# Four edits at stage borders of a transformer block: transposes, a bank, four small loads and the last scaling

## The chip, the cores and the metric

The kernel runs on one core of one Trainium2 chip. A core has a matrix engine (TensorE, PE in the profile, its weight loads PEld), VectorE (DVE), ScalarE (ACT), GpSimd (POOL) and SyncE (SP), which here only issues loads and stores. Each engine works through its own queue in order. The metric is the device time of one execution in microseconds.

## The reference

One streaming encoder block in float32, on 512 tokens of width 1024 and 16 learned meta tokens ahead of them:

```python
xn = rmsnorm(h, norm_mix_g)
proj = xn @ w_in                        # q, k, v of two attention branches
# branch A: stick-breaking attention, 8 heads of 128
# branch B: differential attention, 8 heads: softmax map 1 - lam * softmax map 2
lam = exp(sum(lam_q1 * lam_k1)) - exp(sum(lam_q2 * lam_k2)) + lam_init
gates = sigmoid(xn @ w_gate + b_gate)
h = h + (gates[0] * (o_sb @ w_br_sb) + gates[1] * (o_df @ w_br_df)) @ w_out
hn = rmsnorm(h, norm_ffn_g)
h = h + (silu(hn @ w_ffn_gate) * (hn @ w_ffn_up)) @ w_ffn_down    # 2816 wide
y = rmsnorm(h, norm_final_g)            # meta tokens dropped
```

## The kernel before, in words

**Products in three parts.** Every float32 operand of a large product is split into a rounded part and the rest (`split`, L77 to L81: ScalarE copies the rounded part, `wh` or `hT_h`, and VectorE subtracts it, `wl` or `hT_l`). `mm3` (L293 to L298) then issues three matmuls for one product: high by high (L296), and the two mixed ones (L297, L298).

**Seven products for eight.** Where a product is cut in 2 by 2 blocks, the kernel forms sums of blocks ahead and needs seven block products instead of eight (`a11`, `a12`, `s1` to `s4`, `a22` by their weight side; `b11`, `b21`, `t1` to `t4`, `b22` by their token side). This is done for k and v of the stick-breaking heads from the third on, for the output projection, for SwiGLU's column tiles 2 to 21 of 22, and for the down projection. Several of the seven add into one PSUM bank, and partial sums are copied out of it between them.

**Stages, in order.** Input norm and transposes; eight stick-breaking heads, then eight differential heads (one loop, `br` and `h`), with the projections of the next head issued between the pieces of the present one; gates and merge; output projection (`out_steps`); norm, and transposes of the normed tokens (`turned`, L1145); SwiGLU's column tiles 0 and 1 as plain products (`early_products`); tiles 2 to 21 with seven products each (`first`, `second`, `third`); down projection (`step`), final norm and stores (`finish`, L1406).

**What sets the order.** The program is written out without loops on the chip. A scheduler orders each engine's queue at build time, by a model of time and by the order in the program; `tc.high_priority(offset=EVAC)` moves an instruction up in that order, and `behind(ins, name)` (L83) adds a dependency on an instruction recorded in `cast`. The scheduler sets the waits as well. PSUM banks are taken in turn from two pools: `mm_tile()` (four of 128x512) and `z_tile()` (two of 128x2x512, so two banks each).

**Weights.** `stream` lists all weight pieces in the order of use. `stage_one` (L186 to L210) issues the load of the next into a staging buffer on SP's queue; `generic` (L222) makes the split of one piece, and its argument `after` can put ScalarE's copy behind another instruction. Position `first_ffn` is the gate piece of column tile 2, so `first_ffn - 1` is the up piece of tile 1; `first_down` is the first piece of the down projection.

**The four places of the change.**

- `turned(tp_)` (L1145 to L1166) transposes the normed tokens `hn` for half `tp_` of them (256 tokens, 8 tiles of 128 features, called k; two transposes a k). For two k at a time it issues four transposes into one bank (L1152) and then, for each k, ScalarE's copy to `hT_h` (L1157) and VectorE's rest to `hT_l` (L1158). After the loop `bf` gets a plain copy (L1163) for the block sums. Two z tiles give four banks; k 0 and 1 share one, 2 and 3 the next, and so on. `turned(0)` is issued as soon as the third token tile is normed, among the last steps of the output projection; `turned(1)` comes after the products of gate and up tile 0 with the first 256 tokens.
- `second` and `third` (L1305 to L1334): in column tile f, the products s2, s3 and a22 add into the bank `e1` of `first`, and s1 and s4 into a z bank `e3`. `qx` and `qy` are copies of e1 after s2 and after s3 (L1310, L1315); `qy` then gets e3 added (L1316). The other column tiles issue a22 ahead of s4; the last one, 21, issues s4 first.
- `df_constants` (L818 to L839) loads the four lambda vectors on SP's queue (L822), into a buffer shared with the heads, and computes lambda from them. The loop calls it at stick-breaking head 4.
- `rstd` (L374) gives 1/sqrt from ScalarE's log and exp and one Newton step on VectorE, as three small instructions: u = r*r*v (L388), u = 1.5 - u/2 (L384), r = r*u (L386). `finish(t)` (L1406) calls it, then scales one half of token tile t on VectorE (L1409) and the other on ScalarE (L1411) and issues a store behind each (L1410, L1412). The last call is that of t = 1.

Of the kernel before, what the change touches and what calls it, by code (L numbers as in the profile page):

```python
# [9 lines left out]
F32 = mybir.dt.float32  # L10
# [6 lines left out]
P = 128  # L17
# [4 lines left out]
KT = D // P  # L22
# [19 lines left out]
def block_kernel(ctx: ExitStack, tc: tile.TileContext, x, meta, norm_mix_g, w_in, w_gate, b_gate,  # L42
# [179 lines left out]
    def generic(n):  # L222
        wh, wl = parts(n)
        split(wh, wl, staged[n], nc.gpsimd if n < 3 else None, after="qy" if n == first_down else None)
        cast["split"] = cast["lo"]
# [148 lines left out]
    def rstd(ss, n=1, scale=1.0 / D, more=None):  # L374
# [5 lines left out]

        def newton(steps=(0, 1, 2)):
            for i in steps:
                if i == 1:
                    nc.vector.tensor_scalar(u, u, -0.5, 1.5, op0=ALU.mult, op1=ALU.add)  # L384
                elif i == 2:
                    nc.vector.tensor_tensor(r, r, u, op=ALU.mult)  # L386
                elif n == 1:
                    nc.vector.scalar_tensor_tensor(u, r, r, v, op0=ALU.mult, op1=ALU.mult)  # L388
                else:
                    nc.vector.tensor_tensor(u, r, r, op=ALU.mult)  # L390
                    nc.vector.tensor_tensor(u, u, v, op=ALU.mult)
            return r

# [422 lines left out]
    var_max = const.tile([P, 1], F32, name="var_max")  # L816

    def df_constants():  # L818
        nc.vector.tensor_scalar(g_sub, pcol[:, 32:33], 1.0 - LAM_INIT, None, op0=ALU.mult)
        lam4 = opool.tile([P, 4, 64], F32, tag="sg1", name="lam4")  # L820
        for i, v in enumerate((lam_q1, lam_k1, lam_q2, lam_k2)):
            nc.sync.dma_start(lam4[:, i], v.broadcast_to([P, 64]))  # L822

        lp = opool.tile([P, 2, 64], F32, tag="sg1", name="lp")
        lv = lam4.rearrange("p (a b) c -> p a b c", b=2)
# [167 lines left out]
    for br in range(2):  # L993
# [151 lines left out]
    def turned(tp_):  # L1145
        cs = slice(tp_ * 256, (tp_ + 1) * 256)
        banks = [z_tile() for _ in range(2)]
        for k in range(0, KT, 2):
            pt = banks[k // 2 % 2][:, k // 4]
            for i in range(2):  # L1150
                for t in range(2):
                    nc.tensor.transpose(pt[:, (2 * i + t) * P:(2 * i + t + 1) * P],  # L1152
                                        hn[:, 2 * tp_ + t, (k + i) * P:(k + i + 1) * P], ident)
            for i in range(2):
                g = g_ffn[:, k + i:k + i + 1]
                p = pt[:, i * 256:(i + 1) * 256]
                nc.scalar.activation(hT_h[:, k + i, cs], p, AF.Copy, scale=g)  # L1157
                nc.vector.scalar_tensor_tensor(hT_l[:, k + i, cs], p, g, hT_h[:, k + i, cs].bitcast(F32),  # L1158
                                               op0=ALU.mult, op1=ALU.subtract)
        for k in range(KT):  # L1160
            p = banks[k // 2 % 2][:, k // 4, k % 2 * 256:(k % 2 + 1) * 256]
            if tp_ == 0:
# [101 lines left out]
    with tc.tile_pool(name="ffn", bufs=1) as fp:  # L1264
# [40 lines left out]
        def second(f):  # L1305
# [6 lines left out]
            product(f, "s1", tsum["t1"], e3, True)  # L1312
            product(f, "s3", tsum["t3"], e1, False)
            with tc.high_priority(offset=EVAC):
                cast["qy"] = nc.scalar.copy(qy, e1)  # L1315
                nc.vector.tensor_tensor(qy, e3, qy, op=ALU.add)  # L1316
            return qx, qy

        def third(f, qx, qy):
            e1, e2, e3, sg = bank[f]  # L1320
            def up():
                product(f, "a22", tsum["t4"], e1, False)
                with tc.high_priority(offset=EVAC):
                    nc.vector.scalar_tensor_tensor(aT[:, f, T1], e1, -1.0, sg[:, T1], op0=ALU.mult, op1=ALU.mult)

            def gate_and_up():
                product(f, "s4", tsum["b22"], e3, False)
                with tc.high_priority(offset=EVAC):
                    nc.vector.tensor_tensor(sg[:, T2], e3, qx, op=ALU.add)
                nc.scalar.activation(sg[:, T2], sg[:, T2], AF.Silu)  # L1330
                nc.vector.scalar_tensor_tensor(aT[:, f, T2], qy, -1.0, sg[:, T2], op0=ALU.mult, op1=ALU.mult)

            for half in (up, gate_and_up) if f < NFF - 1 else (gate_and_up, up):
                half()  # L1334

# [69 lines left out]

        def finish(t):  # L1406
            r = rstd(ssq[t][:, 1:2], more=ssq[t][:, 0:1])()
            o = outs[t]
            nc.vector.tensor_scalar(o[:, 0:512], o[:, 0:512], r, None, op0=ALU.mult)  # L1409
            nc.sync.dma_start(ov[:, t, 0:512], o[:, 0:512])  # L1410
            nc.scalar.activation(o[:, 512:D], o[:, 512:D], AF.Copy, scale=r)  # L1411
            nc.sync.dma_start(ov[:, t, 512:D], o[:, 512:D])  # L1412
# [38 lines left out]
        for ph, (w, b, e) in enumerate(DOWN):  # L1451
# [15 lines left out]
            for t in range(2):  # L1467
                for c0, c1 in ((0, 256), (256, 512)) if ph == 6 and t else ((0, 512),):
# [26 lines left out]
                    elif w == "a22":  # L1495
# [3 lines left out]
                        if c1 == 512:  # L1499
                            finish(t)  # L1500
        inner.close()
# [29 lines left out]
```

## Time and profile before

| what | us |
|---|---|
| median of the runs | 933.06 |
| lowest, highest run | 931.36, 1141.8 |
| the profiled execution's own time | 930.84 |
| its span, first to last instruction | 929.1 |
| TensorE busy | 916.9 |
| VectorE, ScalarE, GpSimd busy | 733.4, 583.6, 168.6 |

In the profile a row of the timeline gives the start in us from the span's start, the duration, the engine, the line, the operation with output and inputs, their shape, and in brackets how long the engine had been idle before and what ended that. Matmuls are pipelined, so their durations overlap and one reads their starts. A row of the stretches gives busy time and number of instructions for each engine, the granted TensorE clock, the share of the DMA engines and GB/s. TensorE is busy for all but 12 us of the span: some at the start, some behind the last matmul, the rest at the borders between stages.

### The profile page before, as it was taken

The numbers are of one execution on the slowest core, as the hardware profiler recorded it, in microseconds if no ns is written. First come the engines' busy times: TensorE is split into PE (matmuls) and PEld (weight loads), VectorE is DVE, ScalarE is ACT, GpSimd is POOL, SyncE is SP. The second block draws the span as 40 slices with busy tenths as digits, with TensorE's granted clock in tenths as the row PEclk, the third lists the DMA queues.
The fourth block names the chain that finished last, engine by engine and source line by source line (L and its number), as shares of the span: only waits on it lengthen the run. The fifth ranks groups of instructions, "written<-read, shape, count | busy, mean of one in ns | idle before, by whom it ended". The sixth has DMA issues, their size and how long they took to land.

```text
span 929.1 us, 16027 instructions
## 1 busy us (share of the span) xinstructions
PE 916.9 (99%) x6009; PEld 835.0 (90%) x6010; DVE 733.4 (79%) x1412; ACT 583.6 (63%) x1102; POOL 168.6 (18%) x199
## 2 busy tenths in 40 slices
PE   8999999999999999999999999999999999999997
PEld 5999999998999899998988888899999999988886
DVE  7988877776677766976663787899888889799975
ACT  7665676676666666666665555775555655576554
POOL 4000121222333343344512000001100000000013
PEclk9999999999999999999999999999999999999999
DMA  8525788778777978799987774427754343276642
GB/s 253 143 72 161 167 185 199 177 167 252 192 191 175 220 168 182 183 208 192 194 207 175 220 262 159 126 79 182 172 129 120 93 135 92 92 271 194 191 148 91
DMA packets 155823, 158.41 MB, mean 171 GB/s; under 512 B 6465, under 2 KB 117218, under 8 KB 155746
## 3 DMA queue, kind: packets, MB, share of 16 engines
q1 hardware_dynamic: 132690, 101.61, 36.1%
q0 software_dynamic: 22896, 55.72, 29.3%
q8 instruction: 47, 0.77, 0.3%
q14 instruction: 30, 0.25, 0.1%
q10 hardware_dynamic: 160, 0.07, 0.0%
HBM read 133.64 MB, written 50.86 MB: 199 GB/s over the span
## 4 chain that ended last, share of the span: by engine, by line
PE 94%; DVE 2%; ACT 2%; issue 1%; DMA 0%; ACTq 0%; DVEq 0%
PE mm L296 22%; PE mm L297 22%; PE mm L298 22%; PE z L296 7%; PE z L298 7%; PE z L297 7%; PE z L563 2%; PE z L696 1%; PE z L695 1%; PE tr L537 1%; DVE wl L81 1%; PE z L584 1%; DMA wst<-in_w_ffn_up_dram 0%; DVE hres L1200 0%; PE mm L855 0%
## 5 line engine op out<-in xcount | busy, mean ns | idle before, releaser
L296 PE MATMUL mm<-xT_h,wh 128*128 128x264 f32 (+2 forms) x656 | 213.6, 326 | 0.5 <-ACT xT_h L898 0.5
L297 PE MATMUL mm<-xT_l,wh 128*128 128x264 f32 (+2 forms) x656 | 213.4, 325 | 0.5
L298 PE MATMUL mm<-xT_h,wl 128*128 128x264 f32 (+2 forms) x656 | 212.6, 324 | 0.0
L78 ACT CAST wh<-wst 128x1024 fp32r<-128x1024 f32 (+1 forms) x147 | 141.4, 966 | 77.4 <-PE mm L297 55.5
L81 DVE TENSOR_TENSOR wl<-wst,wh 128x1024 fp32r<-128x1024 f32 (+1 forms) x147 | 163.3, 1116 | 31.2 <-ACT wh L78 30.9
L297 PEld LDWEIGHTS mm<-xT_l,wh 128*128 128x128 f32 x656 | 123.4, 188 | 10.3 <-DVE xT_l L899 1.3
L298 PEld LDWEIGHTS mm<-xT_h,wl 128*128 128x128 f32 x656 | 123.5, 188 | 10.0
L296 PEld LDWEIGHTS mm<-xT_h,wh 128*128 128x128 f32 x656 | 123.4, 188 | 10.0 <-ACT xT_h L898 0.9
L296 PE MATMUL mm<-hT_h,wh 128*128 128x256 f32 x304 | 83.8, 277 | 0.9 <-ACT hT_h L1157 0.8
L298 PE MATMUL mm<-hT_h,wl 128*128 128x256 f32 x304 | 83.9, 277 | 0.0
L297 PE MATMUL mm<-hT_l,wh 128*128 128x256 f32 x304 | 83.8, 276 | 0.0
L296 PEld LDWEIGHTS mm<-hT_h,wh 128*128 128x128 f32 x304 | 56.9, 188 | 1.3 <-ACT hT_h L1157 1.0
L699 DVE CUSTOM_DVE_ANT_0 pr<-z,bias 128x144 f32<-128x144 f32 (+3 forms) x64 | 30.9, 502 | 34.0 <-PE z L696 31.8
L297 PEld LDWEIGHTS mm<-hT_l,wh 128*128 128x128 f32 x304 | 57.0, 188 | 0.0
L298 PEld LDWEIGHTS mm<-hT_h,wl 128*128 128x128 f32 x304 | 57.0, 188 | 0.0
L296 PE MATMUL mm<-o_h,wh 128*128 128x512 f32 x128 | 52.4, 410 | 0.0
L296 PE MATMUL z<-wh,da 128*128 128x512 f32 (+1 forms) x132 | 50.3, 381 | 0.0
L297 PE MATMUL z<-wl,da 128*128 128x512 f32 (+1 forms) x132 | 50.2, 381 | 0.0
L298 PE MATMUL z<-wh,da 128*128 128x512 f32 (+1 forms) x132 | 50.2, 380 | 0.0
L298 PE MATMUL mm<-o_h,wl 128*128 128x512 f32 x128 | 50.1, 391 | 0.0
L297 PE MATMUL mm<-o_l,wh 128*128 128x512 f32 x128 | 49.9, 390 | 0.0
L151 POOL DMA_DIRECT2D ds<-in_w_ffn_down_dram x36 | 30.2, 841 | 91.7 <-ACT wh L78 62.1
(359 smaller groups left out, 2464.5 us busy)
## 6 DMA issues: line engine op xcount, KB each, us to landing
wst<-in_w_in_dram SPq DMA_DIRECT2D x40, 512.0 KB, 6.3
ds<-in_w_ffn_down_dram POOLq DMA_DIRECT2D x30, 512.0 KB, 6.6
wst<-in_w_ffn_gate_dram SPq DMA_DIRECT2D x22, 512.0 KB, 4.0
wsu<-in_w_ffn_up_dram SPq DMA_DIRECT2D x20, 512.0 KB, 4.0
wst<-in_w_gate_dram SPq DMA_DIRECT2D x16, 512.0 KB, 4.8
y_df<-y_out POOLq DMA_DIRECT2D x32, 256.0 KB, 7.7
slots<-ds SPq DMA_DIRECT2D x13, 512.0 KB, 3.3
os<-in_w_out_dram POOLq DMA_DIRECT2D x12, 512.0 KB, 5.2
```

The source lines that it names most:

```text
L78: cast["last"] = (hi_copy or nc.scalar.copy)(hi, src)
L81: cast["lo"] = (lo_eng or nc.vector).tensor_tensor(lo, src, hi.bitcast(F32), op=ALU.subtract)
L151: tc.add_manual_dep(nc.gpsimd.dma_start(dst, src, **kw).ins, cast["last"].ins.name, paced)
L296: nc.tensor.matmul(ps, lhsT=ah, rhs=bh, start=(start and i == 0), stop=False, skip_group_check=skip)
L297: nc.tensor.matmul(ps, lhsT=ah, rhs=bl, start=False, stop=False, skip_group_check=skip)
L298: nc.tensor.matmul(ps, lhsT=al, rhs=bh, start=False, stop=(stop and i == n - 1), skip_group_check=skip)
L537: nc.tensor.transpose(pt[:, j * P:(j + 1) * P], vT[:, j * P:(j + 1) * P], ident)
L563: nc.tensor.transpose(pt[:, (t - j) * P:(t - j + 1) * P], blocks(t, j * P, (j + 1) * P), ident)
L584: nc.tensor.matmul(ps.rearrange("p (t q) -> p t q", q=P)[:, :, lo_rows:P], lhsT=vf[:, 1], rhs=a_s[:, 0:4 * qn], start=False, stop=True)
L695: nc.tensor.matmul(o, lhsT=q[c][:, qs], rhs=k[c][:, 0, k0:k1], start=True, stop=False)
L696: nc.tensor.matmul(o, lhsT=q[c][:, qs], rhs=k[c][:, 1, k0:k1], start=False, stop=True)
L699: nc.vector.tensor_tensor_reduce(po, zz, bb, scale=1.0, scalar=-3.0e38, op0=ALU.add, op1=ALU.max, accum_out=mx[:, t, c:c + 1])
```

## The change

1. `turned(0)` issues all sixteen transposes first and then the eight pairs of copies; `turned(1)` keeps its order of two k at a time. The last `hT_h` copy of `turned(0)` is recorded, and the weight copy of the last piece ahead of `first_ffn` (the up piece of column tile 1) gets a dependency on it.
2. In the last column tile, a22 gets a bank of its own from `mm_tile()`. The copy of e1 after s3 goes to a buffer `qz`; `qy` is e3 plus `qz` as before, VectorE adds the own bank to `qz`, and that sum takes the place of e1 in the last product with the gate. The order is now a22 ahead of s4 in all column tiles.
3. The four lambda loads move into `df_loads`, called at head 2, with buffers of their own; the computation stays at head 4.
4. In the last `finish` both halves are scaled on VectorE, by r and u as two factors, without the step r = r*u; ScalarE takes no part.

```diff
     def generic(n):
         wh, wl = parts(n)
-        split(wh, wl, staged[n], nc.gpsimd if n < 3 else None, after="qy" if n == first_down else None)
+        split(wh, wl, staged[n], nc.gpsimd if n < 3 else None, after={first_down: "qy", first_ffn - 1: "hT"}.get(n))
...
-        def newton(steps=(0, 1, 2)):
+        def newton(steps=(0, 1, 2), factors=False):
+            steps = steps[0:2] if factors else steps
             for i in steps:
...
-            return r
+            return (r, u) if factors else r
...
+    lams = []
+
+    def df_loads():
+        lams.extend((ap_.tile([P, 4, 64], F32, name="lam4"), ap_.tile([P, 2, 64], F32, name="lp")))
+        for i, v in enumerate((lam_q1, lam_k1, lam_q2, lam_k2)):
+            nc.sync.dma_start(lams[0][:, i], v.broadcast_to([P, 64]))
+
     def df_constants():
+        lam4, lp = lams
         nc.vector.tensor_scalar(g_sub, pcol[:, 32:33], 1.0 - LAM_INIT, None, op0=ALU.mult)
-        lam4 = opool.tile([P, 4, 64], F32, tag="sg1", name="lam4")
-        for i, v in enumerate((lam_q1, lam_k1, lam_q2, lam_k2)):
-            nc.sync.dma_start(lam4[:, i], v.broadcast_to([P, 64]))
-
-        lp = opool.tile([P, 2, 64], F32, tag="sg1", name="lp")
...
+            if (br, h) == (0, 2):
+                df_loads()
             if (br, h) == (0, 4):
                 df_constants()
...
     def turned(tp_):
         cs = slice(tp_ * 256, (tp_ + 1) * 256)
         banks = [z_tile() for _ in range(2)]
-        for k in range(0, KT, 2):
-            pt = banks[k // 2 % 2][:, k // 4]
-            for i in range(2):
+        half = [banks[k // 2 % 2][:, k // 4, k % 2 * 256:(k % 2 + 1) * 256] for k in range(KT)]
+        step = 2 if tp_ else KT
+        for k0 in range(0, KT, step):
+            for k in range(k0, k0 + step):
                 for t in range(2):
-                    nc.tensor.transpose(pt[:, (2 * i + t) * P:(2 * i + t + 1) * P],
-                                        hn[:, 2 * tp_ + t, (k + i) * P:(k + i + 1) * P], ident)
-            for i in range(2):
-                g = g_ffn[:, k + i:k + i + 1]
-                p = pt[:, i * 256:(i + 1) * 256]
-                nc.scalar.activation(hT_h[:, k + i, cs], p, AF.Copy, scale=g)
-                nc.vector.scalar_tensor_tensor(hT_l[:, k + i, cs], p, g, hT_h[:, k + i, cs].bitcast(F32),
+                    nc.tensor.transpose(half[k][:, t * P:(t + 1) * P], hn[:, 2 * tp_ + t, k * P:(k + 1) * P], ident)
+            for k in range(k0, k0 + step):
+                g = g_ffn[:, k:k + 1]
+                hi = nc.scalar.activation(hT_h[:, k, cs], half[k], AF.Copy, scale=g)
+                nc.vector.scalar_tensor_tensor(hT_l[:, k, cs], half[k], g, hT_h[:, k, cs].bitcast(F32),
                                                op0=ALU.mult, op1=ALU.subtract)
+                if tp_ == 0:
+                    cast["hT"] = hi
...
+            qz = quarter("q1") if f == NFF - 1 else qy
             with tc.high_priority(offset=EVAC):
-                cast["qy"] = nc.scalar.copy(qy, e1)
-                nc.vector.tensor_tensor(qy, e3, qy, op=ALU.add)
-            return qx, qy
+                cast["qy"] = nc.scalar.copy(qz, e1)
+                nc.vector.tensor_tensor(qy, e3, qz, op=ALU.add)
+            return qx, qy, qz

-        def third(f, qx, qy):
+        def third(f, qx, qy, qz):
             e1, e2, e3, sg = bank[f]
-            def up():
-                product(f, "a22", tsum["t4"], e1, False)
...
-            def gate_and_up():
-                product(f, "s4", tsum["b22"], e3, False)
...
-            for half in (up, gate_and_up) if f < NFF - 1 else (gate_and_up, up):
-                half()
+            own = mm_tile()[:, 0:256] if f == NFF - 1 else None
+            product(f, "a22", tsum["t4"], e1 if own is None else own, own is not None)
+            with tc.high_priority(offset=EVAC):
+                if own is not None:
+                    nc.vector.tensor_tensor(qz, own, qz, op=ALU.add)
+                nc.vector.scalar_tensor_tensor(aT[:, f, T1], e1 if own is None else qz, -1.0, sg[:, T1],
+                                               op0=ALU.mult, op1=ALU.mult)
+            product(f, "s4", tsum["b22"], e3, False)
...
-        def finish(t):
-            r = rstd(ssq[t][:, 1:2], more=ssq[t][:, 0:1])()
+        def finish(t, last=False):
+            r = rstd(ssq[t][:, 1:2], more=ssq[t][:, 0:1])(factors=last)
             o = outs[t]
+            if last:
+                for cs in (D1, D2):
+                    nc.vector.tensor_scalar(o[:, cs], o[:, cs], *r, op0=ALU.mult, op1=ALU.mult)
+                    nc.sync.dma_start(ov[:, t, cs], o[:, cs])
+                return
...
-                            finish(t)
+                            finish(t, t == 1)
```

More of the change, by code (lines that the diff above doesn't have):

```diff
@@ L1147, in turned @@
         banks = [z_tile() for _ in range(2)]
-        for k in range(0, KT, 2):
-            pt = banks[k // 2 % 2][:, k // 4]
-            for i in range(2):
+        half = [banks[k // 2 % 2][:, k // 4, k % 2 * 256:(k % 2 + 1) * 256] for k in range(KT)]
+        step = 2 if tp_ else KT
+        for k0 in range(0, KT, step):
+            for k in range(k0, k0 + step):
                 for t in range(2):
-                    nc.tensor.transpose(pt[:, (2 * i + t) * P:(2 * i + t + 1) * P],
-                                        hn[:, 2 * tp_ + t, (k + i) * P:(k + i + 1) * P], ident)
-            for i in range(2):
-                g = g_ffn[:, k + i:k + i + 1]
-                p = pt[:, i * 256:(i + 1) * 256]
-                nc.scalar.activation(hT_h[:, k + i, cs], p, AF.Copy, scale=g)
-                nc.vector.scalar_tensor_tensor(hT_l[:, k + i, cs], p, g, hT_h[:, k + i, cs].bitcast(F32),
+                    nc.tensor.transpose(half[k][:, t * P:(t + 1) * P], hn[:, 2 * tp_ + t, k * P:(k + 1) * P], ident)
[3 more added lines that the diff above has]
+                nc.vector.scalar_tensor_tensor(hT_l[:, k, cs], half[k], g, hT_h[:, k, cs].bitcast(F32),
                                                op0=ALU.mult, op1=ALU.subtract)
-        for k in range(KT):
-            p = banks[k // 2 % 2][:, k // 4, k % 2 * 256:(k % 2 + 1) * 256]
+                if tp_ == 0:
+                    cast["hT"] = hi
+        for k, p in enumerate(half):
             if tp_ == 0:
@@ L1313, in second @@
             product(f, "s3", tsum["t3"], e1, False)
+            qz = quarter("q1") if f == NFF - 1 else qy
             with tc.high_priority(offset=EVAC):
-                cast["qy"] = nc.scalar.copy(qy, e1)
-                nc.vector.tensor_tensor(qy, e3, qy, op=ALU.add)
-            return qx, qy
-        def third(f, qx, qy):
+                cast["qy"] = nc.scalar.copy(qz, e1)
+                nc.vector.tensor_tensor(qy, e3, qz, op=ALU.add)
+            return qx, qy, qz
+        def third(f, qx, qy, qz):
             e1, e2, e3, sg = bank[f]
-            def up():
-                product(f, "a22", tsum["t4"], e1, False)
-                with tc.high_priority(offset=EVAC):
-                    nc.vector.scalar_tensor_tensor(aT[:, f, T1], e1, -1.0, sg[:, T1], op0=ALU.mult, op1=ALU.mult)
-            def gate_and_up():
-                product(f, "s4", tsum["b22"], e3, False)
[L1328 to L1331, printed above, removed]
-            for half in (up, gate_and_up) if f < NFF - 1 else (gate_and_up, up):
-                half()
+            own = mm_tile()[:, 0:256] if f == NFF - 1 else None
[6 more added lines that the diff above has]
+            product(f, "s4", tsum["b22"], e3, False)
+            with tc.high_priority(offset=EVAC):
+                nc.vector.tensor_tensor(sg[:, T2], e3, qx, op=ALU.add)
+            nc.scalar.activation(sg[:, T2], sg[:, T2], AF.Silu)
+            nc.vector.scalar_tensor_tensor(aT[:, f, T2], qy, -1.0, sg[:, T2], op0=ALU.mult, op1=ALU.mult)
         for f in range(2):
```

## The prediction

> **What bounds the kernel now.** I read the page first, for which engine is busiest (TensorE, nearly all of the span), then the busy time of each engine over eight stretches that cover the span, of which six are shown, then the order in time of the stretches where TensorE is not full.
>
> ```profile
> core 0: us, PE busy (x) PEld busy (x) DVE busy (x) ACT busy (x) POOL busy (x), PEclk, DMA share, GB/s
> ...
> 22.00:588.00 566.00, 565.75 (x3463) 509.81 (x3464) 421.23 (x882) 362.11 (x717) 142.88 (x168) 1.00 0.75 184
> ...
> 598.90:613.00 14.10, 13.18 (x114) 12.78 (x112) 12.23 (x29) 10.29 (x27) 0.00 (x0) 1.00 0.80 219
> 613.00:812.80 199.80, 199.76 (x1762) 199.56 (x1760) 176.77 (x274) 117.38 (x190) 5.79 (x7) 1.00 0.44 118
> 812.80:816.50 3.70, 3.24 (x27) 3.00 (x26) 3.66 (x7) 3.12 (x5) 0.00 (x0) 1.00 0.00 0
> 816.50:922.20 105.70, 105.67 (x497) 88.21 (x495) 92.84 (x139) 65.94 (x105) 10.96 (x8) 1.00 0.57 187
> 922.20:929.10 6.90, 0.00 (x0) 0.00 (x0) 1.66 (x6) 1.73 (x5) 0.72 (x1) 0.82 0.39 152
> ```
>
> TensorE is the bound, at a granted clock of 1.00 wherever it works. Only three of these stretches leave it idle: 0.92 us where SwiGLU's first products start (14.10 less 13.18), 0.46 us at SwiGLU's last product, and the 6.90 us tail after the last matmul. Everywhere else it is full to a few hundredths. The diff takes no matmul away, so it can only win in those three places; their idle time, with the slow first matmul behind each wait, is the whole purse.
>
> **Part 1: the transposes ahead of the copies, and one weight copy put behind them.** This is where the products of SwiGLU's first two tiles begin:
>
> ```profile
> 599.92 0.28 PE L297 MATMUL mm<-hT_l,wh 128*128 128x256 f32 x1
> 600.27 0.66 PE L1152 MATMUL z<-ident,hn 128*128 128x128 f32 x4
> 600.68 0.37 PE L297 MATMUL mm<-hT_l,wh 128*128 128x256 f32 x1
> 600.89 0.60 PE L1152 MATMUL z<-ident,hn 128*128 128x128 f32 x4
> 601.25 0.37 PE L298 MATMUL mm<-hT_h,wl 128*128 128x256 f32 x1
> ...
> 601.31 1.22 DVE L81 TENSOR_TENSOR wl<-wst,wh 128x1024 fp32r<-128x1024 f32 x1
> ...
> 601.67 1.05 ACT L78 CAST wh<-wst 128x1024 fp32r<-128x1024 f32 x1 [1.16 <-DMA wst<-in_w_ffn_up_dram]
> ...
> 601.91 0.28 PE L297 MATMUL mm<-hT_l,wh 128*128 128x256 f32 x1
> 602.02 0.28 PE L298 MATMUL mm<-hT_h,wl 128*128 128x256 f32 x1
> ...
> 602.62 0.83 ACT L1157 ACTIVATE hT_h<-z,pcol 128x256 fp32r<-128x256 f32 x2
> ...
> 603.14 0.39 PE L296 MATMUL mm<-hT_h,wh 128*128 128x256 f32 x1 [0.84 <-ACT hT_h L1157]
> 603.37 0.28 PE L297 MATMUL mm<-hT_l,wh 128*128 128x256 f32 x1
> ...
> 604.79 3.03 ACT L1163 ACTIVATE bf<-z,pcol 128x256 f32<-128x256 f32 x8 [0.19 <-DVE hT_l L1158]
> ```
>
> Starts count here, since the durations overlap. A 256-column matmul takes 0.11 us from start to start (601.91 to 602.02). Four things cost more than that. 599.92 to 600.27 is 0.35, so 0.24 is lost before the second batch of transposes. Each return from transposes to a product is slow: 600.68 to 600.89 is 0.21, 0.10 lost, and I count the same for the return at 601.25. 602.02 to 603.14 is 1.12, so 1.01 is lost, and the matmul after it loses 0.12 more (603.37 less 603.14, less 0.11). Together 1.57 us.
>
> The 1.01 has its cause in the ACT rows. The transposes of tiles 4 to 7 had started by 600.89, but ScalarE, which works in order, stood 1.16 us in front of a weight copy (L78) that waited for its load from w_ffn_up, and then took 1.05 us for that copy; the hT_h copies that TensorE wanted came behind it. The new dependency puts exactly this copy, the last weight copy ahead of SwiGLU's seven-product tiles, behind the last hT_h copy. And with all sixteen transposes issued ahead of the copies, the eight at 600.27 and 600.89 can run with the first eight, which stand among the last matmuls of the output projection. TensorE's work stays the same: 8 x 0.10 us of transposes (0.41 for four, 600.27 to 600.68) move ahead of that projection's end. The end of the output projection moves back by that 0.8 us, and the last token tile's norm behind it; the cover is the 96 products of the first 256 tokens, 96 x 0.11 = 10.6 us, which need only the first two token tiles.
>
> By the PSUM page of the Trainium skill ("PSUM — Partial Sum Buffer", PSUM bank collisions raise a hardware error) engines have to be kept apart by bank, and tiles 4 to 7 lie in other banks than the copies of tiles 0 to 3: by that rule the wait of 0.24 at 600.27 is no bank's but the order of the queue, and nothing says that it goes. The trace shows the wait all the same. By the rule alone this part would give 1.1 where the rows give 1.35.
>
> I take 1.35: the 1.57 less 0.2 for two slow returns that come again elsewhere. Above it lies 1.57. Below it the gain can vanish or turn, in the two ways of the second and third rival.
>
> **Part 2: the last product in its own bank.**
>
> ```profile
> 812.72 0.28 PE L298 MATMUL mm<-hT_h,wl 128*128 128x256 f32 x1
> 813.03 0.37 ACT L1315 COPY qy<-mm 128x256 f32<-128x256 f32 x1
> ...
> 813.45 0.38 PE L296 MATMUL mm<-t_h,wh 128*128 128x256 f32 x1 [0.46 <-ACT qy L1315]
> ...
> 813.67 0.29 PE L297 MATMUL mm<-t_l,wh 128*128 128x256 f32 x1
> ...
> 813.79 0.42 DVE L1316 TENSOR_TENSOR qy<-z,qy 128x256 f32<-128x256 f32 x1
> ...
> 814.13 0.68 DVE L1367 SCALAR_TENSOR_TENSOR da<-aT,da 128x512 fp32r<-128x512 f32 x1
> ...
> 814.73 1.22 DVE L81 TENSOR_TENSOR wl<-wst,wh 128x1024 fp32r<-128x1024 f32 x1
> ...
> 816.49 0.39 PE L296 MATMUL z<-wh,da 128*128 128x512 f32 x1
> ...
> 816.72 0.39 PE L297 MATMUL z<-wl,da 128*128 128x512 f32 x1
> ```
>
> The a22 product adds into the bank that ScalarE is still copying out: 812.72 to 813.45 is 0.73, 0.62 lost, and the next matmul loses 0.11. With a bank of its own a22 starts at 812.83, and its 12 matmuls (1.37 us) carry TensorE to 814.2, when VectorE has read the other bank (813.79 + 0.42 = 814.21); so s4 then waits for next to nothing. TensorE would reach the down projection at 816.49 - 0.73 = 815.76. But its second matmul there needs the first wl, ready at 814.73 + 1.22 = 815.95; it would ask at 815.76 + 0.23 = 815.99 (the pace is 816.72 less 816.49). That just fits, and VectorE has no room: 3.66 of 3.70 us busy in this stretch. The change gives it one add more (the row of L1316, 0.42), and the sum it prepares is ready at 814.2, so the add, and the product behind it (as long), may be queued ahead of that wl. If neither is, the gain is 0.73; if the add is, wl is ready at 816.37 and the gain 0.35; if both are, 816.79, and it is -0.07. I take the middle, 0.35, and keep -0.1 to 0.73.
>
> **Part 3: the lambda loads two heads earlier.**
>
> ```profile
> 77.66 0.37 SPq L210 DMA_DIRECT2D wst<-in_w_br_sb_dram  x1
> 86.25 0.37 SPq L210 DMA_DIRECT2D wsu<-in_w_in_dram  x1
> ...
> 131.79 0.42 SPq L822 DMA_DIRECT2D lam<-in_lam_q_dram  x1
> ...
> 133.96 0.43 SPq L822 DMA_DIRECT2D lam<-in_lam_k_dram  x1
> ```
>
> Four issues take SP from 131.79 to 134.39, 2.6 us. Two heads earlier they stand behind the issue at 77.66 (the load of w_br_sb of that head, the kind of load that stands ahead of them now), and the next one leaves at 86.25: 2.6 us fit into 8.2 us of an idle queue. What they save is a wait of VectorE at head 4. Both lie inside the stretch 22 to 588, where TensorE is busy for 565.75 of 566.00 us. Nothing either way; without that cover the price would be at most the 2.6 us by which weight loads would slip.
>
> **Part 4: the last scaling on VectorE.**
>
> ```profile
> 7.00 0.89 DVE L888 TENSOR_SCALAR xs<-xs,rs 128x512 f32<-128x512 f32 x2
> ...
> 924.26 0.16 DVE L386 TENSOR_TENSOR rs<-rs 128x1 f32<-128x1 f32 x1
> 924.51 0.72 ACT L1411 ACTIVATE outs<-outs,rs 128x512 f32<-128x512 f32 x1 [0.72 <-DVE rs L386]
> 924.52 0.49 DVE L1409 TENSOR_SCALAR outs<-outs,rs 128x512 f32<-128x512 f32 x1
> 925.03 0.33 SPq L1410 DMA_DIRECT2D out_dram<-outs  x1
> 925.46 0.38 SPq L1412 DMA_DIRECT2D out_dram<-outs  x1
> ```
>
> Nothing but the end of the kernel hides this chain, so it counts in full. The step of L386 goes; the first half starts at 924.26 instead of 924.52, and its store leaves at 924.77. The second half now stands behind the first: two such scalings took 0.89 us together (L888), so it is done at 925.15; but SP needs 0.43 from one store to the next (925.03 to 925.46), so it leaves at 925.20. That is 0.26 earlier. No row has a wide scaling with two per-partition factors; if the second factor drops it to the pace of L1367, 0.68 a half, the second store leaves at 925.64, 0.18 later. The nearest row is the scaling with one factor, so I take 0.25 and keep -0.2 to 0.26.
>
> By the VectorE page ("VectorE: DVE Perf Modes", The DRAIN you can't avoid, in the Trainium skill) the second of two VectorE instructions starts only once the first has drained. That would make 0.98 of the 0.89, put the second store at 925.26, and cost 0.06 of the gain. The measured pair decides.
>
> **The sum.** 1.35 + 0.35 + 0 + 0.25 = 1.95 us. The profiled execution took 930.84 us (span 929.1), so the same kind of execution should take 928.9. Other runs of before lie up to the median of 933.06, with 931.36 as the lowest; the middle one of 930.84, 931.36 and 933.06 is 0.5 above the profiled. I add that: 929.4.
>
> **The rivals.**
> *VectorE takes part 2 back.* For it: 3.66 of 3.70 us busy, and an add more. Against it: in the trace the wl at 814.73 came ahead of work of the same tile. TensorE then waits at the first down product for wl instead of for qy: -0.07 in place of 0.35, so 929.8.
> *The first stall changes its name.* Without the 0.24 and the two slow returns TensorE comes to tile 4 at about 602.13 - 0.44 = 601.7. ScalarE, idle from 601.67 - 1.16 = 600.51 on, can have hT_h of two tiles by then (0.83 for two), but hT_l needs VectorE, busy 12.23 of 14.10 us. The program issues hT_l ahead of the wl at 601.31, which is why I count no wait. If that wl stays in front all the same, hT_l begins only at 602.53, TensorE stands for 0.8 us, and part 1 gives 0.55: 930.2. This is also how the change would not do what it says.
> *Slower: the postponed weights come too late.* The copy that is put behind the hT_h copies belongs to the second up tile, and the eight bf copies (L1163, 3.03 us) precede it in the program. Before, it slipped in ahead of them. If it has to queue behind them, the hT_h copies end at 600.51 + 4 x 0.41 = 602.2 at the earliest, bf at 605.2, the copy at 606.2, its wl at 607.5. TensorE has the second pair of tiles in front of it after the 48 products of the first pair. By the groups of the stretch 598.8 to 603.0 it has done 7 of their 16 high-by-high products when it stops:
>
> ```profile
> L296 PE MATMUL mm<-hT_h,wh 128*128 128x256 f32 x7 | 1.6, 280 | 0.0
> ```
>
> Nine are left, 27 matmuls with their mixed parts, 3.0 us from 603.14, so 606.1, less the 1.35: 604.8. If it takes the second gate tile first, that tile's 24 x 0.11 = 2.6 us cover the wait; if gate and up are interleaved, it stands from 604.8 to 607.5: 929.4 + 2.7 = 932.1, against 931.36 for before on the same footing. It decides from a wait of 2.0 us on. Against it: the second pair's weights are needed one after the other in the program, and the scheduler can pull other products forward.
>
> **How the numbers follow.** Forecast 0.5, first rival 0.17, second 0.15, third 0.15; 0.03 for what I don't see. The likeliest case reaches from 928.8 (all upper ends: 1.57 + 0.73 + 0.26 = 2.56) to 930.5. The range holds the rivals too, and a scatter like that of before's runs above (1.7 us over the middle one) and half as much below: 927.4 to 932.6. A measurement of this kernel tells about 2%, 18.6 us, from no change. The whole purse is 2.56 us, and the slower case needs 0.5: same 0.98, faster 0.01, slower 0.01.
>
> **What would show it.** Right: sixteen transposes ahead of the last output product in the profile after, no wait of a product for hT_h, 0.1 us or less of TensorE idle between the last output product and the seven-product tiles; at the last SwiGLU product no wait for L1315's successor; the two last stores 0.2 us nearer to the last matmul. A wait for wl at the first down product shows the first rival; a wait for hT_l there the second; one for wl among the first SwiGLU products the third. I am wrong if TensorE idles elsewhere than before, in the heads or in the down projection: then the order of the queues has changed where the diff did not touch it.

## The result and the profile after

The changed kernel takes 944.5 us (median of 6 runs, 942.55 to 947.69), the kernel before 935.9 us beside it; the ratio is 1.0105 with a 95% interval of 1.0065 to 1.0146. The ratio compares the fast runs alone, so it leaves out one run of the kernel before at 1141.8 us. The forecast was 929.4 us with a range of 927.4 to 932.6: wrong, and on the wrong side. The profiled execution took 947.69 us.

From the page of the kernel after: the span and the busy time of the engines.

```profile
span 945.9 us, 16026 instructions
...
PE 928.4 (98%) x6009; PEld 845.8 (89%) x6010; DVE 734.8 (78%) x1413; ACT 583.1 (62%) x1101; POOL 168.4 (18%) x199
```

TensorE is still the bound, but it is busy 11.5 us longer for the same matmuls and idle 5.3 us longer. Where, the busy time by stretches shows. The borders are the same events in both kernels: I took ScalarE's instructions of one kind and shape in order, the median difference of their starts between the two traces, and moved the borders of before by it. First the rows of the kernel before that were not shown yet, then the kernel after.

```profile
0.00:26.30 26.30, 22.63 (x137) 1.00 0.81 242
...
141.00:167.00 26.00, 26.00 (x170) 1.00 0.80 198
...
598.90:605.00 6.10, 5.18 (x43) 1.00 0.91 257
605.00:640.00 35.00, 35.00 (x312) 1.00 0.43 108
640.00:812.80 172.80, 172.76 (x1524) 1.00 0.46 123
```

```profile
core 0: us, PE busy (x), PEclk, DMA share, GB/s
0.00:31.60 31.60, 24.07 (x137) 0.95 0.70 207
31.60:146.30 114.70, 114.70 (x767) 1.00 0.57 144
146.30:174.30 28.00, 27.06 (x171) 1.00 0.73 185
174.30:606.20 431.90, 431.75 (x2552) 1.00 0.78 191
606.20:611.06 4.86, 4.86 (x38) 1.00 0.74 210
611.06:650.80 39.74, 37.96 (x309) 0.96 0.47 121
650.80:830.25 179.45, 179.45 (x1526) 1.00 0.43 117
830.25:833.35 3.10, 3.10 (x28) 1.00 0.00 0
833.35:939.05 105.70, 105.48 (x495) 1.00 0.54 187
939.05:945.90 6.85, 0.00 (x0) 0.64 0.40 153
```

Lengths after less before: start-up +5.30 (0.31 of it is there from the first instructions on), heads 4 and 5 +2.00, SwiGLU's first products (part 1's place) -1.24, the second half of the same transposes and the tiles behind it +4.74, the seven-product tiles +6.65, the last SwiGLU product -0.60 (0.38 up to the third down product, below), the tail -0.05. The sum is 16.8, which is 945.9 less 929.1. The 6.65 is not the change's: it comes and goes in kernels that have the code of before up to there (below). Without it some 10 us are left in this pair of profiles, and the ratio stands for 9.8 us.

### The profile page after: what moved, and what is told of

It reads as the page before. It is cut to its first block, busy times and chain, and to the rows that moved or that the text cites. A ratio compares the mean times of both kernels' runs of the same rounds, so it can differ in the third digit from the quotient of the medians.

```text
span 945.9 us, 16026 instructions
## 1 busy us (share of the span) xinstructions
PE 928.4 (98%) x6009; PEld 845.8 (89%) x6010; DVE 734.8 (78%) x1413; ACT 583.1 (62%) x1101; POOL 168.4 (18%) x199
## 4 chain that ended last, share of the span: by engine, by line
PE 87%; DVE 6%; DMA 3%; issue 1%; ACT 1%; SPq 0%; DVEq 0%; ACTq 0%
PE mm L297 20%; PE mm L296 20%; PE mm L298 20%; PE z L297 6%; PE z L296 6%; PE z L298 6%; DVE wl L81 2%; PE z L564 1%; DMA wsu<-in_w_in_dram 1%; PE z L697 1%; PE z L696 1%; DMA wst<-in_w_in_dram 1%; PE tr L538 1%; DMA wsu<-in_w_ffn_up_dram 1%; DVE s L638 1%
## 5 line engine op out<-in xcount | busy, mean ns | idle before, releaser
L297 PE MATMUL mm<-hT_l,wh 128*128 128x256 f32 x304 | 86.0, 284 | 0.0
L298 PE MATMUL mm<-hT_h,wl 128*128 128x256 f32 x304 | 85.8, 283 | 0.0
```

The lines of the kernel that those rows point to most:

```text
L297: nc.tensor.matmul(ps, lhsT=ah, rhs=bl, start=False, stop=False, skip_group_check=skip)
L298: nc.tensor.matmul(ps, lhsT=al, rhs=bh, start=False, stop=(stop and i == n - 1), skip_group_check=skip)
```

## The experiments

Each is compared with runs of the kernel before on the same chip; their medians are 937.42 us for the first four experiments of the table, 936.3 for the next four and 934.27 for the last four. The ratio is taken over all runs of both kernels, not from the medians. "Steps" are read from each experiment's profile against the one of the repeated kernel before (span 928.8): the median difference of the starts of ScalarE's and VectorE's like instructions, and how it grows over a place: the start-up (2-14 to 32-80 us), head 2 (to 110-138), heads 4 and 5 (to 170-480), SwiGLU's first products and second transposes together (560-598 to 628-645), the seven-product tiles (to 795-811). The row "after" stands against the profile of before; the row of the repeated kernel shows how far two profiles of one program differ.

| kernel | median, us | ratio [95%] | start | head 2 | heads 4, 5 | SwiGLU's start | tiles |
|---|---|---|---|---|---|---|---|
| after | 944.5 | 1.0105 [1.0065, 1.0146] | 5.01 | 0.00 | 2.00 | 2.91 | 6.92 |
| before, repeated | 938.71 | 1.0011 [0.998, 1.0042] | -0.03 | 0.00 | 0.29 | -0.24 | 0.01 |
| after, repeated | 942.34 | 1.0063 [1.0031, 1.0094] | 6.23 | -0.01 | 3.05 | 1.57 | -0.28 |
| part 3 alone | 938.83 | 1.0032 [1.0, 1.0064] | 3.13 | -0.01 | -0.29 | -0.14 | 2.32 |
| all but part 3 | 941.14 | 1.0033 [1.0006, 1.0059] | 0.01 | -0.01 | 1.26 | 1.85 | 6.84 |
| part 1 alone | 938.55 | 1.0026 [0.9995, 1.0056] | 0.02 | -0.01 | 0.55 | 2.79 | 0.10 |
| part 1 without its tie | 939.6 | 1.0033 [0.9996, 1.0071] | 0.02 | 0.00 | 0.58 | 0.58 | 5.94 |
| part 3, loads held to head 2 | 932.89 | 0.9983 [0.995, 1.0015] | 0.06 | 0.95 | 0.52 | -0.21 | 5.72 |
| part 3, arithmetic held | 931.97 | 0.9992 [0.9957, 1.0026] | 0.05 | 0.00 | -0.29 | -0.07 | 2.33 |
| part 1, block sums held | 933.47 | 0.9991 [0.9964, 1.0018] | 0.06 | -0.01 | 0.33 | 0.08 | 0.39 |
| all, both held | 936.48 | 0.9996 [0.997, 1.0023] | 0.03 | -0.01 | -0.29 | 0.31 | -0.48 |
| part 2 alone | 935.7 | 1.0007 [0.9979, 1.0036] | 0.01 | -0.01 | 1.33 | -0.10 | -0.11 |
| part 4 alone | 933.71 | 1.0003 [0.9979, 1.0027] | 0.02 | -0.01 | 0.15 | 0.40 | 5.59 |

**The two kernels again, and the lambda part taken out or put in alone.** No edits but whole hunks of the diff: the third kernel is the one before with the hunks of `df_loads`, the fourth the changed one without them.

> The kernel before, unchanged, profiled beside the other three on one chip. Two things of the profile after are not explained by the diff's own places: SwiGLU's 256-column matmuls follow each other at 0.118 us where before had 0.113, which adds 6.6 us over the seven-product tiles, and loads in stick-breaking head 4 land later, which adds 2.0 us. Theory (condition of the run): neither comes from the edits; here the kernel before shows on some chips or in some runs a pace of 0.118 too and takes 936 to 939, or all four kernels of this call share one pace. Rival (the edits change the pace): before stays at 0.113 and 931 to 933 here while the run after_again shows 0.118 and 943 to 947.

> The changed kernel again, beside the kernel before on the same chip. Theory (lambda loads): the four lambda loads are issued in the start-up, 10 to 16 us into the span, and VectorE's first lambda instruction stands in front of the third token tile's scaling for 3 to 4 us, so TensorE starts the second half of the tokens 5 us later; with the wait at the second transposes of SwiGLU it is 6 to 9 us slower than before on this chip. Rival (condition of the run): the start costs 5 us but the rest is the chip's, and it is 3 to 5 us slower than before here. If the pace of 0.118 comes with the edits, it is 12 to 15 us slower.

> The kernel before with part 3 alone, the lambda loads. Theory (lambda loads): 5 us slower than before, all of it before 27 us of the span; 7 if the 2 us in head 4 belong to it. Rival (the loss is the transposes'): within 1 us of before, as part 3 was predicted, since everything stands behind a full TensorE.

> The changed kernel without part 3: transposes ahead, own bank, last scaling. Theory (lambda loads): the start is that of before, and the sum of the other three parts is left: 1 to 2 us faster than before if SwiGLU's second transposes do not stand behind a weight load on VectorE, 1 to 2 us slower if they do as in the profile after. Rival (the loss is the transposes'): 4 us or more slower than before.

The slower pace doesn't come with the edits: the repeated kernel after ran its tiles at 0.113, and the twelve runs of the repeated kernel before lie in two groups, four at 930.53 to 934.09 us and eight at 937.67 to 941.45. By its profile the repeated kernel after is 10.7 us slower than the repeated kernel before; over all runs the ratio makes it 5.9 us, just under the 6 to 9 expected.

The start-up's loss goes with part 3 and with nothing else: 3.13 us alone, where 5 were expected, and 0.01 without it. Part 3 is not all: without it 1.85 us are lost where SwiGLU starts. The loads are not at head 2. From SP's order in time in the kernel after:

```profile
10.45 2.42 SPq L824 DMA_DIRECT2D lam<-in_lam_q_dram  x1
12.91 0.43 SPq L824 DMA_DIRECT2D lam<-in_lam_k_dram  x1
...
14.89 0.37 SPq L824 DMA_DIRECT2D lam<-in_lam_q_dram  x1
15.31 0.44 SPq L824 DMA_DIRECT2D lam<-in_lam_k_dram  x1
```

Their buffer was shared with the heads before and is their own now, so I see nothing in the program that holds them back; the build-time order puts them, and the arithmetic that needs only them, into the start-up. (Own buffer and earlier call came together; no run separates the two.) VectorE, which works in order, then stands in front of the last of the four. VectorE and TensorE there, in the order of time:

```profile
20.53 0.29 DVE L830 TENSOR_TENSOR lp<-lam 128x128 f32<-128x128 f32 x1 [3.68 <-DMA lam<-in_lam_k_dram]
...
22.87 0.49 DVE L892 TENSOR_SCALAR xs<-xs,rs 128x512 f32<-128x512 f32 x1
...
23.41 0.48 PE L897 MATMUL z<-ident,xs 128*128 128x128 f32 x1 [4.02 <-DVE xs L892]
23.68 0.42 PE L897 MATMUL mm<-ident,xs 128*128 128x128 f32 x1
23.89 0.42 PE L897 MATMUL z<-ident,xs 128*128 128x128 f32 x1
...
26.30 0.27 PE L897 MATMUL z<-ident,xs 128*128 128x128 f32 x1
26.41 0.27 PE L897 MATMUL mm<-ident,xs 128*128 128x128 f32 x1
```

In the kernel before the same transposes begin so:

```profile
19.23 0.33 PE L893 MATMUL z<-ident,xs 128*128 128x128 f32 x1 [0.16 <-DVE xs L888]
19.40 0.27 PE L893 MATMUL mm<-ident,xs 128*128 128x128 f32 x1
```

The product of the lambda vectors stands 3.68 us; the sums, roots and the scaling of the third token tile are queued behind it; TensorE stands 4.02 us for that scaling (0.16 before), and starts again at half its pace, 0.21 from transpose to transpose until 26.0, then 0.11. By starts: 23.41 less 19.23, less the 0.31 that this trace lies later from its first instructions on, is 3.87; the transposes themselves cost 1.15 more: from their first to the first product behind them it is 3.51 (23.41 to 26.92), 2.36 before (19.23 to 21.59). Sum 5.02. Three profiles with part 3 give the loss at three lengths of the wait: 2.1 us of VectorE's wait cost 3.13, 3.7 cost 5.01, 4.5 cost 6.23. All three have a stretch at half pace behind the wait.

**The loads, or VectorE's place in line?** Two ties on part 3 alone. First the loads held to head 2:

```diff
-            nc.sync.dma_start(lams[0][:, i], v.broadcast_to([P, 64]))
+            behind(nc.sync.dma_start(lams[0][:, i], v.broadcast_to([P, 64])), "last")
```

> The kernel before with part 3 alone, but the four lambda loads tied behind the weight copy that is the last one issued when head 2 begins, so that they and their arithmetic cannot go into the start-up. Theory (the start-up loses because loads with a buffer of their own have nothing to wait for and VectorE then stands in front of them): no loss at 10 to 30 us, the time of the kernel before within 0.5 us all the way. Rival (the fresh buffers cost by where they lie, or by the loads later on): 2 us or more are lost anyway, at head 2 to 4.

The start-up's loss is gone, as the theory has it, but this kernel is not free: 0.95 us at head 2. Its waits there, VectorE's and TensorE's (us in total, times, longest):

```profile
DVE lp L829 <- DMA lam<-in_lam_k_dram: 2.4, 1, 2.4
...
PE mm L296 <- ACT qq L451: 0.7, 1, 0.7
```

The arithmetic follows its loads at once. VectorE stands 2.4 us in front of them again, ScalarE 4.81 us in front of lambda's exp (L832) behind it, and TensorE pays 0.7, a wait that before does not have in that window. SP's next weight load leaves at 87.00 us, where before has 86.09 and this trace lies 0.91 later by then, so SP lost nothing. So the rival had a point: where the diff names the place, the loads are not free either.

Then the loads left free, and only the first arithmetic held to head 4:

```diff
-        nc.vector.tensor_tensor(lp, lv[:, :, 0], lv[:, :, 1], op=ALU.mult)
+        behind(nc.vector.tensor_tensor(lp, lv[:, :, 0], lv[:, :, 1], op=ALU.mult), "last")
```

> Part 3 alone with the loads free (they go into the start-up's SP queue) but the first product of the lambda arithmetic tied behind a weight copy of head 4, so VectorE does not meet it in the start-up. Theory (the loss is VectorE's place in line): the third token tile's scaling is not late, 0 to 0.7 us lost at 10 to 30 us. Rival (the loss is the four issues on SP and their transfers, which push the x and weight loads back): 2 us or more are lost in the start-up as with part 3 alone.

SP's queue in this kernel, and the first of the transposes:

```profile
10.57 2.47 SPq L823 DMA_DIRECT2D lam<-in_lam_q_dram  x1
...
18.92 0.33 PE L896 MATMUL z<-ident,xs 128*128 128x128 f32 x1
```

The loads sit in the start-up as in the changed kernel and the start-up loses 0.05 us. So neither the four issues nor their transfers cost anything; the loss is VectorE's place in line.

**What part 1 does behind its own place.** Part 1 alone, and part 1 without the tie of the weight copy (the `generic` line of before kept).

> The kernel before with part 1 alone (the 16 transposes of turned(0) ahead of the copies, and the weight copy tied behind the last of them). Theory: the tie moves the weight's remainder (wl) and the block sums of the next chunk in front of hT_l in VectorE's order, so VectorE stands in front of the late load of wsu at turned(1). Expected against the kernel before: 0.9 to 1.3 us gained at 600 us, 2 to 4 us lost at 615 to 625 us with the wait for hT_l of turned(1) and the matmuls behind it at half pace; 1 to 3 us slower in all. Rival: the wait at turned(1) comes from the later position that the lambda part leaves behind, not from part 1; then the run is about 1 us faster and shows no such wait.

> Part 1 without its tie: the transposes ahead of the copies, the weight copy of chunk fu 1 free to run where the scheduler puts it. Theory (the tie is the culprit): VectorE's order at turned(1) is that of the kernel before, no wait over 0.5 us for hT_l there, and the gain at 600 us of 0.5 to 1.3 us stays: 0.3 to 1.3 us faster than before. Rival (the gathered transposes themselves are, by pulling the copies and the release of the weight buffers apart, since the order of two loads on SP changes here as well): the wait at turned(1) stays, 1 to 3 us slower.

The gain at 600 us is there: by ScalarE's starts the difference falls by 1.0 in part 1 alone, and by 1.24 in the kernel after. It is given back right behind, at `turned(1)`. Kernel after, VectorE, then TensorE:

```profile
614.98 0.69 DVE L240 TENSOR_TENSOR s<-wsu 128x512 f32<-128x512 f32 x1 [2.17 <-DMA wsu<-in_w_ffn_up_dram]
615.59 1.22 DVE L81 TENSOR_TENSOR wl<-wst,wh 128x1024 fp32r<-128x1024 f32 x1
...
617.33 0.68 DVE L250 TENSOR_TENSOR wsu<-wst,wsu 128x512 f32<-128x512 f32 x1
617.93 0.87 DVE L1163 SCALAR_TENSOR_TENSOR hT_l<-z,pcol,hT_h 128x256 fp32r<-128x256 f32 x2
...
619.49 1.48 PE L1159 MATMUL z<-ident,hn 128*128 128x128 f32 x8 [1.78 <-DVE hT_l L1163]
...
620.98 0.41 PE L298 MATMUL mm<-hT_h,wl 128*128 128x256 f32 x1
621.19 0.41 PE L296 MATMUL mm<-hT_h,wh 128*128 128x256 f32 x1
```

VectorE stands 2.17 us for the load of the next tile's up weights; behind that stand the tied piece's `wl` and two more block sums (L243, L250), and only then `hT_l`, which frees the bank for the next transposes. TensorE idles 1.78 us and goes on at 0.21 a matmul instead of 0.11. Part 1 alone shows the same wait (2.4 us for the load, 1.8 us of TensorE) and the half pace. The repeated kernel after and the one with all but part 3 have the same wait without the half pace. They lose 1.57 and 1.85 us in the column of SwiGLU's start, where the other two lose 2.91 and 2.79.

Without the tie VectorE's order there is that of before, with two `hT_l` ahead of L250; it waits 1.1 us for the load, TensorE 0.6, and 0.58 is lost instead of 2.79. That is neither the gain that my theory expected nor the rival's loss of 1 us and more: most of the loss is the tie's. But the rival had one thing right. With or without the tie, SP's order of two loads changes, and the up weights land at 609.22 and 608.92 us, against 606.74 in the repeated kernel before, so VectorE can meet them early. And the tie has a use: without it TensorE waits 0.3 us for `hT_h`, with it not at all.

Was it the place in line again? The tie kept, and the first block sum held behind the last `bf` instead of behind `hn`:

```diff
-            behind(first, "hn" if f == 2 else "bf")
+            behind(first, "bf")
```

> The kernel before with part 1 whole (tie included), and the first block sum of chunk 2 tied behind the last bf of turned(1) instead of behind hn, so VectorE meets the load of wsu only after all hT_l. Theory (the loss at turned(1) is VectorE standing in front of a load, ahead of hT_l in its order): no wait of TensorE over 1 us for hT_l of turned(1), no half pace behind it; the 1.0 us gained at 600 us stays, so the offset against the kernel before is 0.7 to 1.3 us lower at 640 us than at 590 us. Rival (the tied weight copy itself, whose remainder comes later, makes fu 1 late): the wait moves to wl of fu 1, and 1 us or more is lost at 615 to 630 us.

TensorE's busy time between 610 and 615 us, in part 1 alone and with the sums held:

```profile
610.00:615.00 5.00, 3.00 (x20) 0.88 0.56 159
```

```profile
610.00:615.00 5.00, 5.00 (x44) 1.00 0.35 97
```

The wait and the half pace are gone, though the load still lands as late (608.80 us). But the 1.0 gained at 600 us is not kept as I expected. By TensorE's starts the difference to before goes from 0.13 us at 590 us to -0.92 behind 603, and then back in three places: to -0.46 at the second transposes (606 to 612), to -0.07 at 629.5, and to 0.43 behind 660. The last step has a wait in it, for ScalarE's copy `qx`:

```profile
659.33 0.38 PE L296 MATMUL mm<-hT_h,wh 128*128 128x256 f32 x1 [0.56 <-ACT qx L1310]
```

In the kernel with both ties (below) the same figures are -0.26, -1.29, -0.83, -0.44 and -0.50. In the first two places TensorE is slow between starts without a wait that the profile names; why, no run here shows.

**Both held, and the other two parts alone.** The kernel "all, both held" is the changed one with the arithmetic of part 3 held to head 4 and the sums held behind `bf`.

> The changed kernel with two ties more: the first product of the lambda arithmetic behind a weight copy of head 4, and the first block sum of chunk 2 behind the last bf. Theory (the two orders of VectorE are all that makes the change slow): span 1.2 to 2.0 us under that of the kernel before where both run the SwiGLU tiles at one pace: 0 in the start-up, -1.0 at 600 us, -0.3 to -0.6 at the last SwiGLU product, -0.2 in the tail; by medians 0.996 to 1.002 of before, since the spread of either kernel's runs is wider than the gain. Rival (something else in the change is slow): 3 us or more over the kernel before at one pace.

> The kernel before with part 2 alone (a bank of its own for the last a22 product). Expected by the prediction: 0.35 us gained between the last SwiGLU product and the first down product (0.73 if the add does not stand ahead of wl on VectorE, nothing or 0.07 lost if it stands ahead and wl is late by it), nothing anywhere else. Rival: VectorE's order changes elsewhere too, as with the other parts, and a wait of 1 us or more appears before 830 us.

> The kernel before with part 4 alone (both halves of the last scaling on VectorE with the two factors). Expected by the prediction: the last store issued 0.25 us nearer to the last matmul (from -0.2 to 0.26), the rest of the trace as before. Rival: the two scalings stand behind one another on VectorE and the second store leaves 0.2 us later than before.

With both ties no loss is left to see: ratio 0.9996. Its span is 928.03 us against 928.75 of before where both run the tiles at one pace. That is 0.7 less, short of the 1.2 expected, and 0.29 of it lies in heads 4 and 5, where profiles of one program differ as much; 0.24 lies where SwiGLU starts and 0.20 at the last SwiGLU product. That it beats the kernel before is not shown; the interval of 0.997 to 1.0023 holds both. There is a hint that it does: sorted into the two groups of times (last section), its five runs in the faster group have a mean of 930.5 us against 933.1 of before's eighteen, and its seven in the slower one 937.2 against 938.2. The groups were made after the times were seen, so this would need more runs.

Part 2 alone, kernel with the bank of its own, at the last SwiGLU product and the first down products:

```profile
813.73 0.28 PE L298 MATMUL mm<-hT_h,wl 128*128 128x256 f32 x1
813.85 0.28 PE L296 MATMUL mm<-t_h,wh 128*128 128x256 f32 x1
...
815.74 0.41 DVE L1326 TENSOR_TENSOR q<-mm,q 128x256 f32<-128x256 f32 x1
816.08 1.21 DVE L81 TENSOR_TENSOR wl<-wst,wh 128x1024 fp32r<-128x1024 f32 x1
...
817.34 0.50 PE L297 MATMUL z<-wl,da 128*128 128x512 f32 x1 [0.20 <-DVE wl L81]
817.68 0.39 PE L298 MATMUL z<-wh,da 128*128 128x512 f32 x1
```

From the last s3 matmul to the third down product these are 3.95 us (813.73 to 817.68); before has 4.23 (812.72 to 816.95) in one profile and 4.16 (812.62 to 816.78) in the other. The gain is 0.21 to 0.28; the changed kernel's own 3.85 makes it 0.38. The rival's sign shows too, a wait of TensorE of 1.4 us at head 4, but not its cause: up to 813 us the queues of VectorE, ScalarE, GpSimd and SP have the order of before, so this is scatter between executions. Part 4 alone, the last matmul, the scaling and the stores:

```profile
928.58 0.28 PE L298 MATMUL mm<-wh,da 128*128 128x256 f32 x1
...
931.02 1.00 DVE L1412 TENSOR_SCALAR outs<-outs,rs 128x512 f32<-128x512 f32 x2
...
931.59 0.81 SPq L1413 DMA_DIRECT2D out_dram<-outs  x2
```

The first store leaves 3.01 us behind the last matmul's start, where the repeated kernel before has 3.14 (921.58 to 924.72), and the last store lands 5.70 us behind it instead of 5.84. But the span ends no earlier. From the last matmul's start to the end, first the repeated kernel before, then part 4 alone, each with GpSimd's drain instructions, which belong to the closing steps of the program (shortest, median and longest in ns, then the first and the last start):

```profile
921.58:928.75 7.17, 0.28 (x3) 0.83 0.38 146
L1526 POOLq DRAIN  x3: 50/93/5590, 922.4 to 928.5; - x3
```

```profile
928.58:935.75 7.17, 0.28 (x3) 0.65 0.38 146
L1532 POOLq DRAIN  x3: 50/93/5590, 929.4 to 935.5; - x3
```

It is 7.17 us in both, and in the kernel after. GpSimd's first drain takes 5.59 us and ends 6.37 us behind the last matmul's start in both, later than the last store lands, and the steps that close the program come behind it. So nothing of the 0.25 expected is gained, and none of it could be.

## Why the prediction was wrong

**The step that failed: part 3, "Two heads earlier they stand behind the issue at 77.66 ... Nothing either way."** I placed the loads where the program calls them. The order of a queue goes by dependencies too: the change took away the buffer shared with the heads, which by my reading held these loads (a tie put in its place brings them back to 83.06 us). The four issues went to 10.45 us and, what I did not count at all, the arithmetic behind them went along, ahead of the third token tile's scaling. The cover that I named, TensorE's 565.75 of 566.00 us, belongs to the order of before; the loss fell around 20 us, in a stretch of which I showed nothing (TensorE is busy for 18.44 of before's first 22.00 us). Part 3 was put at nothing and cost 3.13 to 6.23 us. Even at the place that I assumed the loads cost 0.95 us, through the arithmetic and not through SP, whose 8.2 us of an idle queue were there. My price without cover, 2.6 us for late weight loads, was for another mechanism.

**Part 1** had the right mechanism and nearly the right size in its own place: 1.24 us for the 1.35, 1.0 in the repeats; no product waits for `hT_h`, and fourteen of the transposes run in one row (600.18 to 601.93 in the profile after). The rule of the Trainium skill in the prediction ("PSUM — Partial Sum Buffer", PSUM bank collisions raise a hardware error) would have made it 1.1; the rows cannot tell these apart. What was missing was the next consumer. I named a wait for `hT_l` as the second rival and priced it at 0.8 us of TensorE, from a `wl` that stays in front at the same place. It came one step later, at `turned(1)`, with a load in front of it: 1.6 to 2.9 us net, more than the part gives. The third rival, the tied weights coming too late, did not come: TensorE waited 0.2 us for that `wl` in part 1 alone.

**Part 2** went as the middle case: the add stands ahead of `wl`, and the first `wl` product waits 0.20 us. 0.35 was forecast, 0.2 to 0.4 measured. The first rival (-0.07) is out.

**Part 4** gives nothing instead of 0.25. The step that failed is "Nothing but the end of the kernel hides this chain, so it counts in full": GpSimd's drain, 5.59 us, ends 0.53 us behind the landing of the last store of before (6.37 less 5.84), and I never looked at it. The price was off as well: the pair of scalings takes 1.00 us with two factors, where I took 0.89 from the pair with one, and the first store leaves 0.13 earlier instead of 0.26.

**The sum and the range.** "I am wrong if TensorE idles elsewhere than before" was the sentence that came true, and it had 0.03 of the chance. All rivals were variations of the stalls that I had looked at; the range of 5.2 us was built from them and from the scatter of three runs. That no difference of 2% would be seen, which had 0.98, came true: the loss is 1.05%.

**What stays open.** Heads 4 and 5 lost 2.00 and 3.05 us in the two profiles of the whole change. In kernels whose code is that of before up to there they cost between -0.29 and 1.33, and part 3 alone costs -0.29, so up to 1.3 us of it is scatter between executions. In the profile after, VectorE's first sum there waits 12.7 us in two waits for loads from `in_w_in`, 8.0 before; but in the repeated kernel before it waits 11.7 and loses next to nothing. TensorE waits 0.5 and 1.1 us there for ScalarE (L640) in the two profiles of the whole change, and not in those of before. What the rest is was not tried.

## What to carry to other kernels

A buffer of one's own removes a wait and a leash at once: ask what then runs first, and count the consumers of a load as well as its issue. On an engine that works in order, an instruction that waits for a load costs what stands behind it; here it cost 0.05 us to hold the consumer and 0.95 to hold the load. After a tie, look at the order behind the tied instruction as far as the next load that this engine meets. And for the tail, look at what really ends last, the drains of the engines too.

## What the runs showed of the hardware

- **Two paces at a granted clock of 1.00.** In the seven-product tiles the 256-column matmuls follow at 0.113 us in some executions and at 0.118 in others. The two rows of this stretch above show it, 172.76 and 179.45 us busy for the same matmuls (1524 and 1526 in the records). It set in between 610 and 750 us, also in the kernel that does not differ from before up to there (part 4 alone: 5.59 us). This makes two groups of times: of 35 runs of the kernel before beside the last four experiments, 18 lie at 931.84 to 934.27 us and 17 at 936.47 to 940.51. The medians of few runs hang on the mix, which is why the steps above come from profiles. What picks the pace is open.
- **Half pace after a short idle.** Behind 1.78 us without work, the kernel after ran at 0.21 a matmul from 620.62 to 623.32 us (granted clock 0.82 from 617.4 to 627). Part 1 alone did the same behind 1.77 us (granted clock 0.50 from 613.82 to 617.09). Behind the same wait of 1.77 us in the repeated kernel after and in the one with all but part 3 the matmuls followed at 0.12 at once, at a granted clock of 1.00. In part 3 alone TensorE idled 2.39 us in the start-up, went on at full pace for 1.1 us, and only then fell to half (0.50 from 23.07 us on). The Trainium skill ("TensorE: Matmul & The Clock Gate", Part 1: The HAM clock gate) has the clock halved after an idle window of some 3.4 us that runs free of the kernel. That the same idle does and does not trigger it agrees with a window that runs free; that 1.78 us can be enough does not agree with the length.
- **GpSimd's drain at the end.** In all fourteen profiles the first of GpSimd's closing drains takes 5.59 or 5.60 us, and the span ends 7.16 to 7.18 us behind the last matmul's start, whether the last store lands 5.70 us behind it (part 4 in) or 5.83 to 5.84 (not in). What fills the drain is open.
